# Column sums of the norms closer behind their products, six FFN tiles ahead of the second norm, and the right factors in the order of need

## The chip, the cores and the metric

One Trainium2 chip, one core of it. The metric is the device time of one execution in microseconds (us), the median of several runs. TensorE (PE) multiplies and writes into banks of PSUM; VectorE (DVE), ScalarE (ACT) and GpSimd (POOL) work on tiles of 128 partitions in SBUF; SyncE (SP) issues the DMAs.

## The reference

Two layers of a decoder trunk for 1024 tokens of width 1024, all in float32:

```python
for l in range(DEPTH):
    u = rmsnorm(h, attn_norm[l])
    rq, rk, rv, rg, dq, dk, dv = split(u @ w_in[l])
    ret = silu(rg) * rmsnorm(retention_chunkwise(rq, rk, rv), ret_norm[l])
    dif = rmsnorm(diff_attention(dq, dk, dv, lam), diff_norm[l]) * (1.0 - lam_init)
    h = h + concatenate([ret, dif]) @ w_out[l]
    u = rmsnorm(h, ffn_norm[l])
    h = h + (silu(u @ w_gate[l]) * (u @ w_up[l])) @ w_down[l]
return rmsnorm(h, final_norm)
```

`rmsnorm` divides each token by the root of the mean of its squares over the 1024 channels and multiplies by a gain. The hidden width of the FFN is 2816, 22 tiles of 128.

## The kernel before

The kernel keeps h transposed, eight tiles `a` of 128 channels by 1024 tokens, and works on two halves of 512 tokens. A product in float32 is three matmuls: each factor is split in a high part (a cast by ACT) and a low part (source minus high part, by DVE or POOL): high × high, high × low, low × high. `weight`, `wsplit` (L220, L221) do it for weights, `part` (L235, L236) for the right factors.

**Gate and up** use a form with seven products in place of eight (Strassen and Winograd). For each of the 22 tiles of the hidden width, products q0 to q6 of 12 matmuls (128 x 512) run through `gate_up`: q0 (x) and q1 (y) need the first half's norm alone, q2 to q6 the right factors `b[2]` to `b[6]`, which are sums and differences of both halves' norms: t12 and t22 (the second half's norms), b11 and b21 (at first the first half's, in `keep`). `TAGS7` names the pool of tiles for each factor. Products q2, q4 and q6 go on in the bank of x, q3 and q5 in one named z. y lies in a bank "t"; the add `first` (L956) empties it, into tile `kb` or `acc`; ACT copies x (L951), and z between q3 and q5 (L951 too). The weights of the seven products come from `factors`: two raw tiles, four sums on DVE (L903 to L908, in `sums` and `last`), and seven splits.

Since the second half's norm comes late, `feed_forward` runs q0 and q1 of the first `NPRE` tiles ahead: 10 products for which PE needs no second norm. A `Line` holds the products, and `line.later(n, f)` puts an instruction of another engine behind the start of product n. So each engine has a fixed order, that in which the program issues; DVE, ACT and POOL work through their rows one by one.

**The norms** are generators that are woven into the row of matmuls: `yield n` lets n units of matmuls pass (in steps of three) before the norm's next part. `squares` has ACT square the eight tiles (L406) as the products before it update h, and DVE (two of the seven: POOL) add them into one tile `acc` (L414). `rsqrt_rows` then sums over the channels on PE (L378, matmuls with ones), works out the reciprocal root (L383 to L390), and PE transposes it back (L394), `gap` units later. `seven_first` does the first half for the FFN, `seven_second` the second, with the steps of the factors b[2] to b[6] put behind ten products in a fixed order; `norm_half` is the norm ahead of a layer's projection, and `final` the last one.

The last adds to h ahead of a norm are those of the projection (L863, h plus a bank), one for each group of products.

Of the kernel before, what the change touches and what calls it, by code (L numbers as in the profile page):

```python
# [23 lines left out]
HT = T // NH  # L24
# [3 lines left out]
NPRE = 5  # L28
# [3 lines left out]
TAGS7 = ["u", "u", "ka", "v", "sp", "u", "u"]  # L32
# [69 lines left out]
def shape_tables():  # L102
# [10 lines left out]
    kd = np.repeat(np.exp((P - 1 - c)[:, None] * lg[None, :]), 64, axis=1)  # L113
# [31 lines left out]
class Trunk:  # L145
# [29 lines left out]
    def consts(self):  # L175
# [5 lines left out]
        self.tabs = self.const("c_tabs", [P, 1026])  # L181
# [235 lines left out]
    def norm_half(self, h, hf, gcol, us, pool=True, lag=14, first=False, keep=False):  # L417
        nc = self.nc
        sl = slice(hf * HT, hf * HT + HT)
        parts = self.squares(h, sl, 0, pool, first)  # L420
        yield lag
        y = yield from self.rsqrt_rows(parts, D)
        hi = self.t("u", 4, [P, KT, HT], R32)
        lo = self.t("u", 4, [P, KT, HT], R32)
        for k in range(KT):
# [4 lines left out]
            eng = nc.gpsimd if k in ((1, 4) if keep else (1, 3, 5, 7)) else nc.vector  # L430
# [18 lines left out]
    def seven_second(self, h, gcol, b, keep, line):  # L449
# [12 lines left out]
        t2 = []  # L462
# [311 lines left out]
    def ret_scores(self, x, n):  # L774
# [17 lines left out]
        if n < 7:  # L792
# [3 lines left out]
            nc.vector.tensor_tensor(out=kd, in0=tps[:, 0:256], in1=self.tabs[:, 768:1024], op=ALU.mult)  # L796
# [16 lines left out]
    def retention(self, l, x, mix):  # L813
# [3 lines left out]
        st = self.t("acc", 1, [P, 512])  # L817
# [5 lines left out]
        for n in range(8):  # L823
# [13 lines left out]
            if n < 7:  # L837
# [4 lines left out]
                for p in range(2):  # L842
                    for j in range(2):
# [3 lines left out]
                        nc.vector.scalar_tensor_tensor(out=sv, in0=sv, scalar=self.tabs[r, 1024 + p:1025 + p], in1=kv,  # L847
# [39 lines left out]
    def factors(self, line, at, pos, early=0, tags=("wr", "wr"), mixed=False):  # L887
# [44 lines left out]
    def gate_up(self, line, at, b, pre, st, room, done, early=0):  # L932
# [4 lines left out]
        self.factors(line, at, {j: n0 + i for i, j in enumerate([range(7), range(2), range(2, 7)][pre])}, early)  # L937
# [321 lines left out]
```

## Time and profile before

| | us |
|---|---|
| median of 3 runs | 2338.24 |
| lowest, highest | 2337.26, 2345.36 |
| profiled execution | 2341.53 |
| its span | 2339.8 |
| PE busy | 2274.7 |
| DVE busy | 1390.7 |
| ACT busy | 1011.3 |
| POOL busy | 850.9 |

The profile shows one execution; its times count from the span's start. PE's matmuls overlap at their ends, so a matmul listed with 0.39 us starts 0.23 us after the one before. In the timeline, "[idle before <-releaser]" is the time in which the engine stood still ahead of an instruction, and what ended it. The granted clock is 1.00 for the full 2.4 GHz and 0.50 for 1.2 GHz. The FFN of layer 0 begins near 507 us, the boundary of the layers lies near 1180 us, and layer 1's FFN begins near 1661 us.

### The profile page before, as it was taken

What the parts mean: (1) busy time and instruction counts of PE and PEld (TensorE: products, weight loads), DVE (VectorE), ACT (ScalarE), POOL (GpSimd) and SP (SyncE); (2) the same over time, 40 slices, a digit from 0 to 9 for tenths busy, and PEclk for the clock granted to TensorE, in tenths of its full rate; (3) what the DMA queues carried; (4) which work ended last, traced back from release to release, by engine and by line L of the source; (5) the groups of instructions that cost most, each with busy time, mean ns of one, the idle gap of its engine ahead of it and who ended that gap; (6) DMA issues with size and microseconds to landing.
All of it is one profiled execution on the core that took longest, in us unless ns stands there. A gap on an engine that the chain in (4) does not pass through costs nothing. (4 is left out here: it accounts for less than half of the span.)

```text
span 2339.8 us, 30724 instructions
## 1 busy us (share of the span) xinstructions
PE 2274.7 (97%) x11328; PEld 1906.9 (82%) x11328; DVE 1390.7 (59%) x2512; ACT 1011.3 (43%) x1905; POOL 850.9 (36%) x672
## 2 busy tenths in 40 slices
PE   7999999997999999999999999999889999999998
PEld 5888898876888888888888888988768888888887
DVE  7777603968543433896557774058874444449855
ACT  5666623434333333543246665244443333345332
POOL 4111212144545455335231112212544545544351
PEclk8999999999999999999999999999999999999999
DMA  4312121101332322753232122111123232345522
GB/s 159 81 46 64 46 91 45 55 28 56 125 126 77 126 86 92 242 164 115 73 90 55 49 70 81 56 36 54 46 94 128 77 126 77 104 145 184 185 63 73
DMA packets 73926, 215.66 MB, mean 92 GB/s; under 512 B 7984, under 2 KB 10032, under 8 KB 73776
## 3 DMA queue, kind: packets, MB, share of 16 engines
q1 hardware_dynamic: 73776, 213.70, 28.5%
q8 instruction: 89, 1.46, 0.3%
q14 instruction: 61, 0.50, 0.1%
HBM read 161.24 MB, written 44.04 MB: 88 GB/s over the span
## 5 line engine op out<-in xcount | busy, mean ns | idle before, releaser
L221 POOL TENSOR_TENSOR w<-wr,w 128x512 fp32r<-128x512 f32 x302 | 430.3, 1437 | 497.9 <-ACT w L220 466.3
L261 POOL TENSOR_TENSOR w<-wr,w 128x512 fp32r<-128x512 f32 x140 | 186.6, 1339 | 576.4 <-ACT w L260 547.5
L268 PE MATMUL ps_mm<-u,w 128*128 128x512 f32 (+1 forms) x735 | 296.6, 404 | 0.0
L270 PE MATMUL ps_mm<-u,w 128*128 128x512 f32 (+1 forms) x735 | 288.0, 392 | 0.0
L269 PE MATMUL ps_mm<-u,w 128*128 128x512 f32 (+1 forms) x735 | 287.8, 392 | 0.0
L220 ACT CAST w<-wr 128x512 fp32r<-128x512 f32 x320 | 193.2, 619 | 154.3 <-DVE wr L905 74.7
L244 PE MATMUL ps_mm<-u,w 128*128 128x512 f32 x448 | 175.6, 392 | 5.6 <-DVE t L963 5.6
L246 PE MATMUL ps_mm<-u,w 128*128 128x512 f32 x448 | 174.8, 390 | 0.0
L245 PE MATMUL ps_mm<-u,w 128*128 128x512 f32 x448 | 174.8, 390 | 0.0
L270 PEld LDWEIGHTS ps_mm<-u,w 128*128 128x128 f32 x735 | 138.4, 188 | 30.4
L951 ACT COPY t<-ps_mm 128x512 f32<-128x512 f32 x80 | 47.0, 588 | 258.6 <-PE ps_mm L246 258.6
L268 PEld LDWEIGHTS ps_mm<-u,w 128*128 128x128 f32 x735 | 138.8, 189 | 24.1
L269 PEld LDWEIGHTS ps_mm<-u,w 128*128 128x128 f32 x735 | 138.8, 189 | 23.3
L260 ACT CAST w<-wr 128x512 fp32r<-128x512 f32 x140 | 86.0, 619 | 128.8 <-PE ps_t L269 38.5
L305 PE MATMUL ps_mm<-w,u 128*128 128x256 f32 x448 | 127.1, 284 | 1.0 <-DVE u L431 1.0
L303 PE MATMUL ps_mm<-w,u 128*128 128x256 f32 x448 | 127.9, 285 | 0.0
L304 PE MATMUL ps_mm<-w,u 128*128 128x256 f32 x448 | 126.8, 283 | 0.0
L863 DVE TENSOR_TENSOR a<-a,ps_mm 128x512 f32<-128x512 f32 (+1 forms) x148 | 98.7, 667 | 45.7 <-PE ps_mm L270 27.5
L577 DVE CUSTOM_DVE_ANT_0 sp<-ps_s,wr 128x512 f32<-128x512 f32 (+2 forms) x192 | 103.2, 551 | 34.3 <-PE ps_s L575 33.1
L581 ACT ACTIVATE sp<-sp,m 128x256 f32<-128x256 f32 (+7 forms) x128 | 99.2, 775 | 53.4 <-DVE m L580 52.9
L244 PE MATMUL ps_t<-u,w 128*128 128x512 f32 x256 | 104.2, 407 | 18.5 <-DVE kb L956 18.5
L903 DVE TENSOR_TENSOR t<-wr,wr 128x512 f32<-128x512 f32 x48 | 35.4, 737 | 123.0 <-DMA wr<-wts 123.0
(364 smaller groups left out, 5959.8 us busy)
## 6 DMA issues: line engine op xcount, KB each, us to landing
wr<-wts SPq DMA_DIRECT2D x192, 512.0 KB, 3.7
mx<-s_fast SPq DMA_DIRECT2D x56, 512.0 KB, 5.2
s_fast<-mx SPq DMA_DIRECT2D x48, 512.0 KB, 4.3
kb<-ka SPq DMA_DIRECT2D x64, 128.0 KB, 2.3
s_rest<-mx SPq DMA_DIRECT2D x12, 512.0 KB, 2.9
kb<-wts SPq DMA_DIRECT2D x12, 512.0 KB, 5.4
mx<-s_rest SPq DMA_DIRECT2D x12, 512.0 KB, 3.3
a<-xT SPq DMA_DIRECT2D x16, 256.0 KB, 5.4
```

The source lines that it names most:

```text
L220: nc.scalar.copy(h, src)
L221: (eng or nc.gpsimd).tensor_tensor(out=o, in0=src, in1=h.bitcast(F32), op=ALU.subtract)
L244: mm(ps, lhsT=wh[:, c], rhs=bh, start=first and i == 0, stop=False, skip_group_check=True)
L245: mm(ps, lhsT=wh[:, c], rhs=bl, start=False, stop=False, skip_group_check=True)
L246: mm(ps, lhsT=wl[:, c], rhs=bh, start=False, stop=i == 3, skip_group_check=True)
L261: nc.gpsimd.tensor_tensor(out=o, in0=raw[:, cols], in1=h.bitcast(F32), op=ALU.subtract)
L268: mm(out, lhsT=lh, rhs=rh, start=first, stop=False)
L269: mm(out, lhsT=lh, rhs=rl, start=False, stop=False)
L270: mm(out, lhsT=ll, rhs=rh, start=False, stop=last)
L303: mm(o, lhsT=uh, rhs=wh, start=k == 0, stop=False)
L304: mm(o, lhsT=uh, rhs=wl, start=False, stop=False)
L305: mm(o, lhsT=ul, rhs=wh, start=False, stop=k == KT - 1)
```

## The change

- In the FFN's norms the column sums come 12 matmuls behind the products (11 units in steps of three) where they were 33 and 18, and the transposes 9 behind them where they were 15 and 9; in the norm at the layers' boundary it is 12 and 9 where it was 15 and 15.
- POOL adds no squares; DVE adds all. `acc` has two buffers. In `norm_half` behind the first, all low parts are DVE's.
- `NPRE` is 6. x of the sixth tile lies in a bank "s"; y of the last two tiles have a bank each that is taken once ("t" and "s", `hold`), and the z of the first six tiles share the one named "s".
- `seven_second` issues its steps by the need of the products, three and then four behind each product; the low parts of t22 are DVE's.
- The raw tiles of the first full tile of weights and their sums come at the start of the FFN, and the low parts of seven named products' weights are DVE's (`own`).
- The decay table of the retention's keys is read with a broadcast (4 columns in place of 256).

```diff
-NPRE = 5
+NPRE = 6
...
-TAGS7 = ["u", "u", "ka", "v", "sp", "u", "u"]
+TAGS7 = ["u", "u", "ka", "v", "u", "u", "sp"]
...
-            s = (tmp() if k else self.t("acc", 1, [P, 512]))[:, :n]
+            s = (tmp() if k else self.t("acc", 2, [P, 512]))[:, :n]
...
-                    eng = nc.gpsimd if pool and k in (2, 4) else nc.vector
-                    eng.tensor_tensor(out=acc, in0=acc, in1=s, op=ALU.add)
+                    nc.vector.tensor_tensor(out=acc, in0=acc, in1=s, op=ALU.add)
...
+        parts = self.squares(h, sl, 0, True, first)
         yield lag
-        y = yield from self.rsqrt_rows(parts, D)
+        y = yield from self.rsqrt_rows(parts, D, gap=gap)
...
-            eng = nc.gpsimd if k in ((1, 4) if keep else (1, 3, 5, 7)) else nc.vector
+            eng = nc.gpsimd if keep and k in (1, 4) else nc.vector
...
-        parts = self.squares(h, slice(0, HT), 0, True)
-        yield 32
-        y = yield from self.rsqrt_rows(parts, D)
+        parts = self.squares(h, slice(0, HT), 0)
+        yield 11
+        y = yield from self.rsqrt_rows(parts, D, gap=9)
...
-        parts = self.squares(h, sl, 0, True)
-        yield 16
+        parts = self.squares(h, sl, 0)
+        yield 11
...
-        b += [self.views(tag) for tag in TAGS7[2:4]]
...
+        b += [self.views(TAGS7[2]), self.views(TAGS7[3]), None, self.views(TAGS7[5]), None]
+        two = [self.big("sp") for _ in range(2)]
+        t2 = [two[i // 2][:, c[i % 2]] for i in range(4)]
...
+        def sub(out, x, z, q=None, i=0):
+            v(out=out, in0=x, in1=z, op=ALU.subtract)
+            if q is not None:
+                nc.scalar.copy(b[q][i][0], out)
...
-            b22 = self.views(TAGS7[5])
-            for i in range(4):
-                norm(t22[i], 4 + i)
-                self.part(t22[i], b22[i], nc.gpsimd)
-            yield
...
-                low(t2[i], b[2][i])
-                nc.scalar.copy(b[3][i][0], b11[i])
-            yield
-            for i in range(4):
-                low(b11[i], b[3][i])
-            yield
-            for i in range(4):
-                v(out=b21[i], in0=b21[i], in1=t2[i], op=ALU.subtract)
-            yield
-            b.append(self.views(TAGS7[4]))
-            for i in range(4):
-                v(out=b11[i], in0=t22[i], in1=t12[i], op=ALU.subtract)
-                nc.scalar.copy(b[4][i][0], b11[i])
...
-        go = steps()
-        for q in range(10):
-            line.later(line.n + q, lambda: next(go))
+        r = range(4)
+        ops = [lambda i=i: norm(t12[i], i) for i in r]
+        ops += [lambda i=i: norm(t22[i], 4 + i) for i in r]
+        for i in r:
+            ops.append(lambda i=i: sub(b11[i], t12[i], b11[i]))
+            ops.append(lambda i=i: sub(t2[i], t22[i], b11[i], 2, i))
+        ops += [lambda i=i: low(t2[i], b[2][i]) for i in r]
+        ops += [lambda i=i: self.part(b11[i], b[3][i], nc.vector) for i in r]
...
+        ops += [lambda i=i: sub(b11[i], t22[i], t12[i]) for i in r]
+        ops += [lambda i=i: self.part(t22[i], b[5][i], nc.vector) for i in r]
+        ops.append(lambda: room(4))
+        ops += [lambda i=i: self.part(b11[i], b[4][i], nc.vector) for i in r]
+        ops += [lambda i=i: sub(b21[i], b21[i], t2[i]) for i in r]
+        ops.append(lambda: room(6))
+        ops += [lambda i=i: self.part(b21[i], b[6][i], nc.vector) for i in r]
+        for i, op in enumerate(ops):
+            line.later(line.n + (i // 3 if i < 21 else 7 + (i - 21) // 4), op)
...
-            line.w[n] = self.wsplit(src, self.nc.vector if mixed and n % 3 == 0 else None)
+            line.w[n] = self.wsplit(src, self.nc.vector if n in own else None)
...
-            put(pos[2] - 4 - early, load, 0)
-            put(pos[2] - 3 - early, load, 1)
-            put(pos[2] - 1 - early, sums)
-            put(pos[2] - 1 - early, last)
+            n = pos[2] - LEAD
+            n0, n1, n2 = early or (n - 4, n - 3, n - 1)
+            line.later(n0, lambda: load(0))
+            line.later(n1, lambda: load(1))
+            line.later(n2, sums)
+            line.later(n2, last)
...
-                    st[name] = self.bank(tag)
+                    st[name] = st.pop("bank_" + name, self.bank)(tag)
...
-        tiles = {}
+        tiles, held = {}, {}
+
+        def hold(tag):
+            if tag not in held:
+                held[tag] = self.bank(tag)
+            return held[tag]
...
-            st[t]["tag"] = ["mm", "mm", "mm", "o", "t"][t]
+            st[t]["tag"] = ["mm", "mm", "mm", "o", "t", "s"][t]
             self.gate_up(line, at + 2 * t, b, 1, st[t],
-                         lambda t=t: g[t] if t < 4 else self.t("acc", 1, [P, 512]), None)
+                         lambda t=t: g[t] if t < 4 else self.t("acc", 2, [P, 512]), None, own=range(4, 2 * NPRE, 2))
+            if t > 3:
+                st[t]["bank_y"] = lambda tag, t=t: hold("ts"[t % 2])
+            st[t]["bank_z"] = hold
...
+            kw = {"early": (-1, -1, 0), "tags": ("sp", "sp"), "own": range(2 * NPRE, 2 * NPRE + 5, 2)} if t == 0 else {}
+            self.gate_up(line, at + 2 * t, b, 2 if t < NPRE else 0, st[t], room, done(t), **kw)
...
-        norm0 = self.norm_half(h, 0, 0, us, False, keep=True)
-        norm1 = self.norm_half(h, 1, 0, us, False, 8, True)
+        norm0 = self.norm_half(h, 0, 0, us, keep=True, gap=14)
+        norm1 = self.norm_half(h, 1, 0, us, 8, 14, True)
```

PE, ahead of the FFN of layer 0: L378 are the column sums of the first half, ps_mm the groups of the projection that end with an add to h. Before:

```order
2449 L268 MATMUL ps_mm_865_4776<-u_682_3876,w_829_4581 128x512
2450 L269 MATMUL ps_mm_865_4776<-u_683_3877,w_829_4581 128x512
2451 L270 MATMUL ps_mm_865_4776<-u_682_3876,w_830_4582 128x512
2452 L378 MATMUL ps_s_867_4787<-c_ones_74,acc_855_4725 128x1 x4
2453 L268 MATMUL ps_mm_865_4776<-u_682_3876,w_829_4581 128x512
2454 L269 MATMUL ps_mm_865_4776<-u_683_3877,w_829_4581 128x512
2455 L270 MATMUL ps_mm_865_4776<-u_682_3876,w_830_4582 128x512
2456 L268 MATMUL ps_mm_869_4803<-u_682_3876,w_831_4585 128x512
```

and now:

```order
2428 L268 MATMUL ps_mm_863_4748<-u_682_3876,w_824_4571 128x512
2429 L269 MATMUL ps_mm_863_4748<-u_683_3877,w_824_4571 128x512
2430 L270 MATMUL ps_mm_863_4748<-u_682_3876,w_825_4572 128x512
2431 L378 MATMUL ps_s_865_4762<-c_ones_74,acc_855_4725 128x1 x4
2432 L268 MATMUL ps_mm_867_4775<-u_682_3876,w_826_4575 128x512
2433 L269 MATMUL ps_mm_867_4775<-u_683_3877,w_826_4575 128x512
2434 L270 MATMUL ps_mm_867_4775<-u_682_3876,w_827_4576 128x512
2435 L268 MATMUL ps_mm_867_4775<-u_682_3876,w_826_4575 128x512
```

The sums stood 33 matmuls behind the last group of their half (its end is row 2418 of before), now 12; that is 21 places.

DVE, in the FFN of layer 0: L956 of before and L940 of now is the same add, which empties the bank of y (kb_876 is the place of tiles 2 and 3, acc that of tile 4). L469 of before is the low part of a factor, L496 and L500 differences; now L469 are differences, L474 and L236 low parts of factors and L221 those of weights. Before:

```order
771 L956 TENSOR_TENSOR kb_876_4907<-ps_t_935_5111,t2_934_5109 128x512
772 L469 TENSOR_TENSOR ka_914_5021<-sp_932_5101,ka_912_5019 128x512 x2
773 L469 TENSOR_TENSOR ka_915_5022<-sp_933_5102,ka_913_5020 128x512 x2
774 L469 TENSOR_TENSOR v_918_5025<-mx_841_4607,v_916_5023 128x512 x2
775 L469 TENSOR_TENSOR v_919_5026<-mx_842_4608,v_917_5024 128x512 x2
776 L956 TENSOR_TENSOR kb_876_4907<-ps_t_942_5162,t2_941_5160 128x512
777 L496 TENSOR_TENSOR mx_843_4609<-mx_843_4609,sp_932_5101 128x512 x2
778 L496 TENSOR_TENSOR mx_844_4610<-mx_844_4610,sp_933_5102 128x512 x2
779 L500 TENSOR_TENSOR mx_841_4607<-u_911_5018 128x512 x2
780 L500 TENSOR_TENSOR mx_842_4608<-u_911_5018 128x512 x2
781 L956 TENSOR_TENSOR acc_958_5240<-ps_t_951_5211,t2_950_5209 128x512
```

and now:

```order
781 L940 TENSOR_TENSOR kb_876_4907<-ps_t_936_5105,t2_935_5103 128x512
782 L221 TENSOR_TENSOR w_941_5141<-wr_934_5096,w_940_5140 128x512
783 L469 TENSOR_TENSOR sp_920_5022<-u_909_5011,mx_842_4608 128x512
784 L474 TENSOR_TENSOR ka_912_5014<-sp_919_5021,ka_910_5012 128x512 x2
785 L474 TENSOR_TENSOR ka_913_5015<-sp_920_5022,ka_911_5013 128x512 x2
786 L236 TENSOR_TENSOR v_916_5018<-mx_841_4607,v_914_5016 128x512
787 L940 TENSOR_TENSOR kb_876_4907<-ps_t_943_5150,t2_942_5148 128x512
788 L221 TENSOR_TENSOR w_948_5186<-sp_888_4930,w_947_5185 128x512
789 L236 TENSOR_TENSOR v_916_5018<-mx_841_4607,v_914_5016 128x512
790 L236 TENSOR_TENSOR v_917_5019<-mx_842_4608,v_915_5017 128x512 x2
791 L469 TENSOR_TENSOR mx_841_4607<-u_909_5011 128x512 x2
792 L469 TENSOR_TENSOR mx_842_4608<-u_909_5011 128x512 x2
```

Between the adds of y of tiles 2 and 3 stood eight low parts; now there are one low part of a weight, one difference, four low parts of ka and one of v.

ACT, a little later: L951 of before and L935 of now copy x (ps_mm) and z (ps_s) of the first full tile. L507 of before and L235 of now are casts of factors, L220 of weights. Before:

```order
477 L507 CAST u_962_5263<-mx_843_4609 128x512 x2
478 L507 CAST u_962_5263<-mx_844_4610 128x512 x2
479 L951 COPY t2_963_5272<-ps_mm_896_4953 128x512
480 L336 ACT_TABLE_LOAD
481 L336 ACTIVATE kb_875_4906<-kb_875_4906 128x512
482 L220 CAST w_965_5288<-wr_945_5179 128x512
483 L951 COPY t2_967_5296<-ps_s_964_5275 128x512
```

and now:

```order
482 L935 COPY t2_968_5304<-ps_mm_898_4957 128x512
483 L336 ACT_TABLE_LOAD
484 L336 ACTIVATE kb_875_4906<-kb_875_4906 128x512
485 L220 CAST w_969_5319<-wr_953_5215 128x512
486 L235 CAST sp_971_5323<-mx_843_4609 128x512 x2
487 L235 CAST sp_972_5324<-mx_844_4610 128x512
488 L935 COPY t2_975_5333<-ps_s_961_5252 128x512
```

The copy of z stands behind the first three casts of the seventh factor now (sp_971 and sp_972); before, behind those of the sixth.

## Rows read from the trace of the kernel before

**Rows 1.** The page, busy us (share of the span) and instructions of an engine.
```profile
PE 2274.7 (97%) x11328; PEld 1906.9 (82%) x11328; DVE 1390.7 (59%) x2512; ACT 1011.3 (43%) x1905; POOL 850.9 (36%) x672
```

**Rows 2.** Waits of PE: engine line waited for: us, times, longest.
```profile
PE ps_t L244 <- DVE kb L956: 18.5, 4, 5.1
PE ps_s L378 <- DVE acc L414: 12.1, 6, 3.5
PE ps_mm L244 <- DVE t L963: 5.6, 2, 2.8
```

**Rows 3.** Windows by stage: stretch, length, busy (instructions) PE PEld DVE ACT POOL, clock, DMA.
```profile
511.00:569.50 58.50, 44.30 (x166) 34.82 (x164) 51.98 (x63) 27.05 (x49) 31.58 (x20) 0.85 0.16 47
1665.00:1724.00 59.00, 44.28 (x172) 34.43 (x171) 54.84 (x65) 27.05 (x49) 31.63 (x20) 0.88 0.18 50
569.50:700.00 130.50, 130.25 (x571) 107.28 (x572) 60.13 (x84) 45.89 (x82) 62.99 (x46) 1.00 0.35 121
```

**Rows 4.** Windows behind five waits of PE, same columns.
```profile
514.00:520.50 6.50, 6.50 (x22) 5.52 (x23) 1.35 (x5) 1.59 (x5) 4.66 (x4) 0.50 0.18 42
541.20:544.50 3.30, 3.30 (x10) 2.56 (x9) 3.30 (x5) 3.30 (x7) 1.92 (x2) 0.50 0.07 27
548.00:554.70 6.70, 4.45 (x11) 3.48 (x12) 6.70 (x10) 1.47 (x3) 1.04 (x1) 0.50 0.27 78
569.60:576.00 6.40, 6.25 (x27) 5.18 (x28) 3.73 (x7) 1.59 (x3) 1.30 (x1) 1.00 0.42 145
1179.50:1186.00 6.50, 5.45 (x17) 4.71 (x18) 1.56 (x5) 0.41 (x2) 3.72 (x4) 0.50 0.72 245
```

**Rows 5.** PE's instructions: start, us, line, tiles, count, [idle before, releaser].
```profile
491.92 0.95 PE L378 MATMUL ps_s<-c_ones,acc 128*128 128x1 f32 x8
511.46 0.39 PE L246 MATMUL ps_t<-u,w 128*128 128x512 f32 x1
513.93 1.41 PE L378 MATMUL ps_s<-c_ones,acc 128*128 128x1 f32 x6 [2.08 <-DVE acc L414]
540.52 0.50 PE L244 MATMUL ps_t<-u,w 128*128 128x512 f32 x1 [4.14 <-DVE kb L956]
550.25 0.79 PE L244 MATMUL ps_t<-u,w 128*128 128x512 f32 x1 [5.12 <-DVE kb L956]
569.75 0.50 PE L244 MATMUL ps_mm<-u,w 128*128 128x512 f32 x1 [2.80 <-DVE t L963]
1180.55 1.84 PE L378 MATMUL ps_s<-c_ones,acc 128*128 128x1 f32 x8 [3.48 <-DVE acc L414]
```

**Rows 6.** DVE's instructions, same columns.
```profile
486.07 0.69 DVE L414 TENSOR_TENSOR acc<-acc,t 128x512 f32<-128x512 f32 x1 [0.75 <-ACT t L406]
511.25 0.67 DVE L863 TENSOR_TENSOR a<-a,ps_mm 128x512 f32<-128x512 f32 x1
516.87 0.16 DVE L390 SCALAR_TENSOR_TENSOR ny<-nx,ny 128x4 f32<-128x4 f32 x1
520.70 2.72 DVE L465 SCALAR_TENSOR_TENSOR u<-a,c_gains,ps_s 128x512 f32<-128x512 f32 x4 [1.44 <-PE ps_s L394]
543.89 5.70 DVE L469 TENSOR_TENSOR v<-mx,v 128x512 fp32r<-128x512 f32 x4
550.12 2.48 DVE L496 TENSOR_TENSOR mx<-mx,sp 128x512 f32<-128x512 f32 x4
569.02 0.68 DVE L963 TENSOR_TENSOR t<-ps_mm,t 128x512 f32<-128x512 f32 x1
1174.04 3.47 DVE L414 TENSOR_TENSOR acc<-acc,t 128x512 f32<-128x512 f32 x2 [0.88 <-POOL acc L414]
```

**Rows 7.** POOL's low parts, one alone and the first of three beside DVE.
```profile
487.88 1.29 POOL L221 TENSOR_TENSOR w<-wr,w 128x512 fp32r<-128x512 f32 x1 [7.74 <-ACT w L220]
544.20 1.51 POOL L221 TENSOR_TENSOR w<-wr,w 128x512 fp32r<-128x512 f32 x1 [1.38 <-ACT w L220]
```

**Rows 8.** ACT's copy out of the bank of z.
```profile
561.17 0.58 ACT L951 COPY t<-ps_s 128x512 f32<-128x512 f32 x1
```

More of the change, by code (lines that the diff above doesn't have):

```diff
@@ L396, in rsqrt_rows, with squares @@
         return out[:, :cols]
-    def squares(self, h, sl, alone, pool, first=False):
+    def squares(self, h, sl, alone, kb=False, first=False):
         nc = self.nc
-        tmp = (lambda: self.big("kb")[:, 0:512]) if first else self.tmp
+        tmp = (lambda: self.big("kb")[:, 0:512]) if kb else self.tmp
         n = sl.stop - sl.start
@@ L412, in squares, with norm_half @@
                 else:
-                    eng = nc.gpsimd if pool and k in (2, 4) else nc.vector
-                    eng.tensor_tensor(out=acc, in0=acc, in1=s, op=ALU.add)
+                    nc.vector.tensor_tensor(out=acc, in0=acc, in1=s, op=ALU.add)
         return parts
-    def norm_half(self, h, hf, gcol, us, pool=True, lag=14, first=False, keep=False):
+    def norm_half(self, h, hf, gcol, us, lag=11, gap=9, first=False, keep=False):
         nc = self.nc
         sl = slice(hf * HT, hf * HT + HT)
-        parts = self.squares(h, sl, 0, pool, first)
+        parts = self.squares(h, sl, 0, True, first)
         yield lag
-        y = yield from self.rsqrt_rows(parts, D)
+        y = yield from self.rsqrt_rows(parts, D, gap=gap)
         hi = self.t("u", 4, [P, KT, HT], R32)
@@ L795, in ret_scores @@
                 nc.tensor.transpose(out=tps[:, P * p:P * p + P], in_=rk[p][:, cs], identity=self.ident)
-            nc.vector.tensor_tensor(out=kd, in0=tps[:, 0:256], in1=self.tabs[:, 768:1024], op=ALU.mult)
+            heads = lambda t: t.rearrange("p (h c) -> p h c", h=4)
+            nc.vector.tensor_tensor(out=heads(kd), in0=heads(tps[:, 0:256]),
+                                    in1=heads(self.tabs[:, 768:772]).broadcast_to([P, 4, 64]), op=ALU.mult)
         return sd, kd
@@ L816, in retention @@
         mm = nc.tensor.matmul
-        st = self.t("acc", 1, [P, 512])
+        st = self.t("acc", 2, [P, 512])
         nc.gpsimd.memset(st, 0.0)
@@ L846, in retention @@
                         sv = state[p][r, P * j:P * j + P]
-                        nc.vector.scalar_tensor_tensor(out=sv, in0=sv, scalar=self.tabs[r, 1024 + p:1025 + p], in1=kv,
+                        nc.vector.scalar_tensor_tensor(out=sv, in0=sv, scalar=self.tabs[r, 772 + p:773 + p], in1=kv,
                                                        op0=ALU.mult, op1=ALU.add)
@@ L885, in out_diff, with factors @@
                     yield from self.down_group(h, w, f, hf, 4, rhs, "mm")
-    def factors(self, line, at, pos, early=0, tags=("wr", "wr"), mixed=False):
+    def factors(self, line, at, pos, early=None, tags=("wr", "wr"), own=()):
         v = self.nc.vector.tensor_tensor
@@ L930, in factors, with gate_up @@
             put(pos[6], split, pos[6], 1, 1)
-    def gate_up(self, line, at, b, pre, st, room, done, early=0):
+    def gate_up(self, line, at, b, pre, st, room, done, **kw):
         nc = self.nc
@@ L936, in gate_up @@
         n0 = len(line.products)
-        self.factors(line, at, {j: n0 + i for i, j in enumerate([range(7), range(2), range(2, 7)][pre])}, early)
+        self.factors(line, at, {j: n0 + i for i, j in enumerate([range(7), range(2), range(2, 7)][pre])}, **kw)
         def go(name, tag, q):
@@ L1075, in down_fast @@
         for e in range(2):
-            self.factors(line, at + 2 * e, {j: n0 + 2 * j + e for j in range(7)}, 0,
-                         [RAWS[(m + e) % 5], RAWS[(m + 2 + e) % 5]], True)
+            self.factors(line, at + 2 * e, {j: n0 + 2 * j + e for j in range(7)}, None,
+                         [RAWS[(m + e) % 5], RAWS[(m + 2 + e) % 5]],
+                         [n for n in range(n0, n0 + 14) if n % 3 == 0])
         def go(st, name, tag, q, n):
@@ L1170, in final @@
         sl = slice(c0, c0 + n)
-        parts = self.squares(h, sl, alone, True)
+        parts = self.squares(h, sl, alone)
         yield 14
```

31 lines of the change are left out of this document (4 added, 27 removed).

## The prediction

> **What bounds the kernel now.** I read the busy table first: PE works 97% of a span of 2339.8 us [rows 1], so a gain can only come from the places where PE stands still or runs slowly. The list of PE's waits shows them: adds of squares that column sums wait for (L378), adds that empty the banks of y (L956), and one add of the first full tile (L963) [rows 2]. Then the windows by stage. In the middle of the FFN, 571 matmuls take 130.5 us, a pace of 0.2285 us, 2.74 us for a product of 12 [rows 3]. The first 58.5 us of layer 0's FFN hold 166 matmuls, 12 of them column sums and transposes of about 1.5 us together: 154 × 0.2285 + 1.5 = 36.7 us of work, so 21.8 us are lost; layer 1's 59 us hold 172, 38.1 us of work, and lose 20.9 us [rows 3]. PE's single instructions and the granted clock say how. Four waits of 2.08, 4.14, 5.12 and 2.80 us make 14.1 us [rows 5], and after three of them the clock is granted at 0.50, the 1.2 GHz level, for 6.50, 3.30 and 4.45 us of busy time, half of which is lost: 7.1 us [rows 4]. Together 21.2 us, which agrees. At the boundary of the layers a wait of 3.48 us [rows 2] and half of 5.45 us at 0.50 [rows 4] make 6.2 us.
>
> So the change touches 21.8 + 20.9 + 6.2 = 48.9 us, and a little at the end. All of these waits end with a DVE instruction. DVE is busy for 51.98 of the 58.5 us [rows 3]; what orders its queue decides.
>
> **Column sums 11 units behind the products.** For the first half of layer 0 the sum moves 21 matmuls forward (33 to 12): 491.92 − 21 × 0.2285 = 487.12 [rows 5]. Its last add of squares ends at 486.07 + 0.69 = 486.76 [rows 6], so it need not wait. The transposes behind it come 4.8 + 1.4 = 6.2 us earlier (9 matmuls behind the sum, not 15), and with them the 16 norm instructions of that half. They stood among the last adds of the projection: the one at 511.25 [rows 6] came 3.7 us after its group on PE, which ended 18 matmuls before the sum's place at 511.69 (last matmul 511.46 + 0.23 [rows 5]), at 507.6. Freed, it ends at 508.4, and with the 0.75 us to the next add of squares and that add's 0.69 us [rows 6] the sum of the second half is ready at 509.8. Its place moves 6 matmuls to 510.3. That would be no wait, but the two squares that POOL added now stand on DVE too (1.4 us). I take 0.8 us, with bounds of 0 and the present 2.08.
>
> **Steps by need, on a fuller DVE.** From 520.70 to 569.02 DVE now does 52 instructions in 48.3 us, 0.93 us each. Without company one costs 0.68 us (2.72/4, read from a bank) or 0.62 us (2.48/4, SBUF alone) [rows 6]. The rest is POOL: four subtractions that took 5.70 us stood beside three low parts on POOL [rows 6, 7], (5.70 − 2.48)/3 = 1.07 us each. The new queue, from the first low part behind the norm to the last low part of the seventh factor, has 65: 44 steps (four more, since POOL gives up the parts of t22), 7 low parts of weights that were POOL's, 8 sums of weights and 6 adds of y. It starts about 2.2 us behind the sum's place, at 512.5 (now the sum starts at 513.93 and the last row of the statistics ends at 517.03, 3.1 us, half of them at half clock [rows 5, 6]). POOL has about 7 low parts left in that time.
>
> Who waits, with the products of this FFN counted from 0, of which 0 lies ahead of the sum, and with PE's places counted from 510.3 (product n starts at 510.3 + (n − 1) × 2.74 + 1.55, the sum and the transposes):
> - Product 9, y of tile 4, takes the bank that the add of y of tile 3 empties. That add is the 33rd instruction: 512.5 + 8 × 0.68 + 25 × 0.62 + 3 × 1.07 = 536.7, against a place at 533.8: 2.9 us. Now products 8 and 9 wait 4.14 and 5.12 us [rows 5].
> - Product 13, the first z, takes the bank of y of tile 5, whose add is the 52nd: 512.5 + 5.4 + 44 × 0.62 + 6 × 1.07 = 551.6, against 544.7.
> - Product 15 needs the first z copied out by ACT, which in ACT's queue stands behind casts that wait for the last subtractions, DVE's 61st: 512.5 + 5.4 + 53 × 0.62 + 7 × 1.07 = 558.3, and 1.2 us for cast and copy (the copy is 0.58 [rows 8]): 559.5, against 550.2.
>
> Each takes in the one before, so the sum is 559.5 − 550.2 = 9.3 us, with 0.8 for the column sum. What half clock comes before product 15 hides in its wait; behind it I add 2.0 us, the mean of what followed the five waits here (3.25, 1.65, 2.2, 0 and 2.7 us of loss [rows 4]). That makes 12.1 us against 21.8 and 20.9: gains of 9.7 and 8.8 us.
>
> By bounds: without any company the 61st ends at 550.8, which leaves product 15 a loss of 1.8, with the column sum 2.6 and with half clock up to 5; at today's 0.93 us each it ends at 569.2, a loss of 20.2 + 2.8 = 23.0 us.
>
> On POOL's price the Trainium skill ("SBUF — State Buffer", section "SBUF: two separate sides") says that the port pair that DVE and GpSimd share is locked for a whole instruction and the other blocks. By that rule a POOL low part would cost DVE its full 1.29 us alone [rows 7], not the 1.07 us above: 1.5 us more per layer, 3 us in all. The rows bear out the direction and not the full size.
>
> **Boundary, ends, the rest.** At the boundary two adds of squares took 3.47 us from 1174.04 on, behind an add on POOL [rows 6]. On DVE alone at 0.69 each they would end at 1175.4 with the same start, and the last add of the projection, 0.67 behind them, and the last add of squares (0.75 + 0.69 later) at 1177.5; without the 0.88 us of idle time for POOL, at 1176.6. The sum's place is 1180.55 − 3.48 − 3 × 0.2285 = 1176.4 [rows 5]. That leaves 0.2 to 1.1 us of waiting; I take 0.8, and 0.5 for a clock that may fall: 1.3 against 6.2, a gain of 4.9. At the program's end two POOL adds leave the chain of the squares: 0.5 us, between 0 and 1.3 (a POOL instruction alone is 1.29 [rows 7]); at its start POOL added no squares, and I count nothing. The decay table read with a broadcast keeps its one DVE instruction, and attention's other waits stay; I cost them at nothing, between −1 and +1 us. One bank for z in six tiles gives a copy or add one or two products' time (2.74 or 5.5 us) for 0.58 to 0.68 us of work [rows 6, 8]: nothing, unless DVE is late.
>
> **The sum.** 9.7 + 8.8 + 4.9 + 0.5 = 23.9 us. The profiled execution took 2341.5 us (span 2339.8), 3.3 above the median of 2338.2: 2341.5 − 23.9 = 2317.6 for a profiled run, and 2338.2 − 23.9 = 2314 as median.
>
> **Rivals.**
> A. DVE runs nearly undisturbed, and the clock does not fall: losses of about 5 per FFN, −16.8 − 15.9 − 5.4 = −38, so 2300. For it: a 2.80 us wait at 569.75 was followed by full clock [rows 4, 5]. Against: three others of like length were not.
> B. The shortening of the queue is eaten: DVE stays at 0.93 us an instruction, because adds wait in turn for PE's products and lows for ACT's casts. 23.0 per FFN loses 3.3 us, and the boundary and the end gain 5.4: 2336, no change. At 0.85 us it is 18.2 per FFN: 2326. For it: 13 more instructions. Against: POOL's share of the contention falls by more than half.
> C. DVE becomes the bound, on the slower side. While three POOL instructions ran, an instruction took 1.43 us [rows 6]. If moved casts and lows wait for one another in DVE's strict row so that its mean is 1.05 us, the 61st ends at 576.6 and FFN loses 27.6 + 2.8 = 30.4 us: 8.6 + 9.5 − 5.4 = +13, so 2351. It decides from 0.95 us on (24.3 us lost per FFN, 2.5 + 3.4 more, which eat the 5.4). Against: all the pairs with POOL would have to stay.
> D. The early sums of the norm wait for their adds, as 3.48 us does now, since they stand closer behind the products: all six at 2 us and half clock after each lose about 2 us more than forecast at four places, +8: 2322.
>
> On the clock: of the four waits in layer 0's first window, the one of 2.80 us was followed by full clock and the three others by 0.50 [rows 4, 5]. The Trainium skill ("TensorE: Matmul & The Clock Gate", section "HAM oscillation — how this bites in real kernels") describes this as a cost that is paid anew at each idle gap long enough to cool the engine. By that rule all three new waits would be followed by half clock; what follows products 9 and 13 vanishes in the next wait, and behind product 15 it would be 2.7 us, 0.7 us a layer more than above.
>
> **How the numbers follow.** Forecast 0.55; A 0.17; B 0.14 (half of it at 2326 and half at 2336); C 0.05; D 0.09. Leaving out the upper part of B, C and the fast tail of A gives 2300 to 2328. What a measurement can tell here is about 0.5%, 11.7 us: faster means below 2326.5. The forecast, A, D and a little of B lie there: 0.85; same 0.10, the rest of B and of D; slower 0.05, C.
>
> **What would show it right or wrong.** Right: the waits on L956's successor shrink to one of about 3 us per layer, with one on the z bank and one on ACT's copy behind it; the column sums wait under 1 us at four places; the first FFN window has about 12 us less than full pace, not 21.8; DVE's 65 instructions take about 48 us. Wrong: a mean DVE instruction over 0.85 us there, a new wait on the bank of z in each tile, or half clock for over 6 us behind the last wait.

## The result and the profile after

The changed kernel takes 2317.4 us (median of 4 runs, 2316.4 to 2319.02) against 2339.34 us of the kernel before (median of 4): ratio 0.9903, 95% interval 0.9883 to 0.9923, 22 us or 0.9% less. Forecast were 2314 and a gain of 24. The total came out near, but by terms that missed in both directions.

The page, and the waits of PE that answer to [rows 2] (engine, line waited for: us in total, times, longest):

```profile
PE 2265.0 (98%) x11328; PEld 1900.0 (82%) x11328; DVE 1389.3 (60%) x2564; ACT 1010.4 (44%) x1905; POOL 781.0 (34%) x620
```
```profile
PE ps_s L378 <- DVE acc L413: 8.2, 4, 4.1
PE ps_t L244 <- ACT t L935: 5.7, 2, 2.8
...
PE ps_s L244 <- DVE acc L940: 3.4, 2, 2.5
PE ps_s L244 <- ACT t L935: 3.4, 2, 1.7
...
PE ps_mm L244 <- DVE t L947: 1.1, 2, 0.6
```

The 18.5 us on the adds that empty y's banks, L956 of before, are gone; 5.7 + 3.4 + 3.4 + 1.1 us stand in the same stretch. The line of the column sums, 12.1 us before, still has 8.2: 4.06 at the boundary, the rest at the program's start and end. PE's and ACT's single instructions in layer 0's FFN, at the boundary, and products 9 and 13 of layer 1 (1677.84 and 1691.48), against [rows 5]:

```profile
509.51 1.02 PE L378 MATMUL ps_s<-c_ones,acc 128*128 128x1 f32 x8
...
535.78 0.47 PE L244 MATMUL ps_t<-u,w 128*128 128x512 f32 x1 [2.84 <-ACT t L935]
...
549.41 0.47 PE L244 MATMUL ps_s<-v,w 128*128 128x512 f32 x1 [0.89 <-DVE acc L940]
...
556.82 0.50 PE L244 MATMUL ps_s<-u,w 128*128 128x512 f32 x1 [1.70 <-ACT t L935]
...
560.40 0.50 PE L244 MATMUL ps_mm<-sp,w 128*128 128x512 f32 x1 [0.56 <-DVE t L947]
...
1166.06 1.20 PE L378 MATMUL ps_s<-c_ones,acc 128*128 128x1 f32 x5 [4.06 <-DVE acc L413]
...
1677.84 0.47 PE L244 MATMUL ps_t<-u,w 128*128 128x512 f32 x1 [2.85 <-ACT t L935]
...
1691.48 0.47 PE L244 MATMUL ps_s<-v,w 128*128 128x512 f32 x1 [2.52 <-DVE acc L940]
...
556.19 0.58 ACT L935 COPY t<-ps_s 128x512 f32<-128x512 f32 x1
```

The column sum at 509.51 waits for nothing now. Products 9, 13, 15 and 16 of layer 0 wait 2.84, 0.89, 1.70 and 0.56 us. At the boundary the sum waits 4.06 us, more than the 3.48 of before. DVE's row in the same FFN, from the first low part behind the norm to the add behind the last low part, against [rows 6]:

```profile
511.63 0.17 DVE L390 SCALAR_TENSOR_TENSOR ny<-nx,ny 128x4 f32<-128x4 f32 x1
511.75 0.69 DVE L221 TENSOR_TENSOR w<-wr,w 128x512 fp32r<-128x512 f32 x1
...
534.95 0.68 DVE L940 TENSOR_TENSOR kb<-ps_t,t 128x512 f32<-128x512 f32 x1
...
548.59 0.68 DVE L940 TENSOR_TENSOR acc<-ps_s,t 128x512 f32<-128x512 f32 x1
...
552.64 3.59 DVE L469 TENSOR_TENSOR mx<-mx,sp 128x512 f32<-128x512 f32 x4
556.15 3.59 DVE L236 TENSOR_TENSOR sp<-mx,sp 128x512 fp32r<-128x512 f32 x4
559.66 0.68 DVE L947 TENSOR_TENSOR t<-ps_mm,t 128x512 f32<-128x512 f32 x1
```

The row of 65 instructions runs from 511.75 to 559.66: 47.9 us, 0.74 us each. Before, 52 took 48.3 us.

To see where the time went, take the distance from each matmul to the next, less the usual (median) distance behind a matmul of that line and shape, and add up what exceeds 0.15 us (time lost by PE, us):

| | start | FFN 0 | boundary | FFN 1 | end | all |
|---|---|---|---|---|---|---|
| before | 13.5 | 21.0 | 5.6 | 20.8 | 2.9 | 83.6 |
| after | 10.0 | 8.3 | 6.0 | 8.5 | 3.9 | 56.4 |

The losses shrink by 27.2 us and the span by 25.2 (2339.8 to 2314.6); the difference was not traced. The two FFNs give 25.0 of it, the start 3.5; the boundary and the end give nothing and take 1.4.

### The profile page after: what moved, and what is told of

Same layout as the page of the kernel before. It is cut to its first block, busy times and chain, and to the rows that moved or that the text cites. A ratio compares the mean times of both kernels' runs of the same rounds, so it can differ in the third digit from the quotient of the medians.

```text
span 2314.6 us, 30688 instructions
## 1 busy us (share of the span) xinstructions
PE 2265.0 (98%) x11328; PEld 1900.0 (82%) x11328; DVE 1389.3 (60%) x2564; ACT 1010.4 (44%) x1905; POOL 781.0 (34%) x620
## 4 chain that ended last, share of the span: by engine, by line
PE 82%; DVE 12%; ACT 3%; issue 2%; DMA 1%; POOL 0%; SPq 0%; DVEq 0%; ACTq 0%; POOLq 0%
PE ps_mm L244 8%; PE ps_mm L246 8%; PE ps_mm L245 8%; PE ps_mm L268 7%; PE ps_mm L269 7%; PE ps_mm L270 7%; PE ps_s L244 5%; PE ps_s L246 5%; PE ps_s L245 5%; PE ps_mm L305 2%; PE ps_mm L303 2%; PE ps_mm L304 2%; PE ps_t L246 2%; PE ps_t L245 2%; PE ps_t L244 2%
## 5 line engine op out<-in xcount | busy, mean ns | idle before, releaser
L221 POOL TENSOR_TENSOR w<-wr,w 128x512 fp32r<-128x512 f32 x286 | 401.9, 1417 | 532.1 <-ACT w L220 492.1
L261 POOL TENSOR_TENSOR w<-wr,w 128x512 fp32r<-128x512 f32 x140 | 184.7, 1326 | 576.9 <-ACT w L260 550.5
L220 ACT CAST w<-wr 128x512 fp32r<-128x512 f32 x312 | 188.1, 619 | 134.5 <-DVE wr L887 72.0
L245 PE MATMUL ps_mm<-u,w 128*128 128x512 f32 x432 | 168.3, 390 | 0.0
L246 PE MATMUL ps_mm<-u,w 128*128 128x512 f32 x432 | 168.2, 389 | 0.0
L244 PE MATMUL ps_mm<-u,w 128*128 128x512 f32 x432 | 168.2, 389 | 0.0
L935 ACT COPY t<-ps_mm 128x512 f32<-128x512 f32 x76 | 44.6, 587 | 254.0 <-PE ps_mm L246 254.0
L260 ACT CAST w<-wr 128x512 fp32r<-128x512 f32 x140 | 85.9, 619 | 133.9 <-PE ps_mm L269 42.8
L244 PE MATMUL ps_s<-u,w 128*128 128x512 f32 x264 | 102.9, 390 | 3.4 <-ACT t L935 3.4
```

Source lines behind the costliest of these rows:

```text
L220: nc.scalar.copy(h, src)
L221: (eng or nc.gpsimd).tensor_tensor(out=o, in0=src, in1=h.bitcast(F32), op=ALU.subtract)
L244: mm(ps, lhsT=wh[:, c], rhs=bh, start=first and i == 0, stop=False, skip_group_check=True)
L245: mm(ps, lhsT=wh[:, c], rhs=bl, start=False, stop=False, skip_group_check=True)
L246: mm(ps, lhsT=wl[:, c], rhs=bh, start=False, stop=i == 3, skip_group_check=True)
L261: nc.gpsimd.tensor_tensor(out=o, in0=raw[:, cols], in1=h.bitcast(F32), op=ALU.subtract)
```

## The experiments

Each was timed in three rounds beside the kernel before; the medians and these losses of PE (as in the table above) came out. The runs were made in three sets; the kernel before took 2340.3, 2339.8 and 2339.9 us beside them and 2339.3 beside the changed kernel, so the sets are compared as they stand, to about 1 us:

| run | us | FFN 0 | boundary | FFN 1 | end |
|---|---|---|---|---|---|
| own_pool | 2322.95 | 11.9 | 6.1 | 10.7 | 3.9 |
| own_all | 2324.94 | 10.9 | 6.2 | 11.7 | 3.9 |
| lows_pool | 2315.72 | 8.5 | 5.8 | 9.1 | 3.9 |
| bw_dve | 2314.16 | 9.1 | 1.7 | 8.4 | 3.9 |
| before_places | 2341.04 | 20.6 | 5.6 | 20.5 | 2.9 |
| before_sq_only | 2339.82 | 21.6 | 4.8 | 20.9 | 2.8 |
| before_sq | 2330.49 | 17.8 | 5.8 | 17.6 | 2.9 |
| old_places | 2324.48 | 12.7 | 6.1 | 12.6 | 3.9 |
| old_steps | 2324.40 | 12.7 | 5.8 | 12.0 | 4.1 |
| npre5 | 2334.03 | 16.8 | 6.0 | 15.3 | 4.0 |
| best1 | 2312.26 | 8.4 | 1.7 | 9.1 | 2.9 |
| best3 | 2316.11 | 9.9 | 1.7 | 10.5 | 2.9 |

**What the low parts cost on which engine: own_pool, own_all.**

```diff
-  own=range(4, 2 * NPRE, 2)           "own": range(2 * NPRE, 2 * NPRE + 5, 2)
+  (own_pool) none of them on DVE
+  (own_all)  own=range(3, 2 * NPRE)   "own": range(2 * NPRE, 2 * NPRE + 5)
```

> The changed kernel with the low parts of the weights of seven products at the FFN's start back on POOL, all else as changed. Theory 1 (the FFN's start is bound by DVE's row, in which a low part on DVE costs 0.62 us and one on POOL costs DVE about 1.1 us by contention): the row loses 7 x 0.62 = 4.3 us and gains 7 x 1.1 = 7.7, so product 16 starts 3.4 us later in each layer: +7 us, 2324. Rival (DVE's number of instructions counts, POOL's work is free): 4.3 us less in each layer, 2309.

> The changed kernel with the low parts of all weights of products 3 to 16 on DVE, none on POOL in the stretch of the FFN's start. Theory 1: about 7 low parts leave POOL, 7 x (1.1 - 0.62) = 3.4 us less in DVE's row per layer: 2311. Rival (number of DVE's instructions): 7 x 0.62 = 4.3 us more per layer: 2326.

own_pool lost 5.5 us to the changed kernel, as theory 1 has it (+7) and against the rival (−8). own_all lost 7.5 us: theory 1 expected a gain, and the rival's number, 2326, is the nearer one. Two things in its DVE row speak against counting a price of 1.1 us for each POOL instruction. A low part of a weight now stands among the adds of squares ahead of the second half's sum (first line). And in a strict row a low part waits for ACT's cast, and the row with it (the other two); the row of layer 0 takes 49.0 us in place of 47.9.

```profile
501.80 1.77 DVE L221 TENSOR_TENSOR w<-wr,w 128x512 fp32r<-128x512 f32 x1
...
530.14 0.69 DVE L221 TENSOR_TENSOR w<-wr,w 128x512 fp32r<-128x512 f32 x1 [1.69 <-ACT w L220]
...
536.36 0.69 DVE L221 TENSOR_TENSOR w<-wr,w 128x512 fp32r<-128x512 f32 x1 [0.49 <-ACT w L220]
```

In layer 0 the loss is the sum's: it costs 1.7 us (0.3 in the changed kernel) and 1.5 us of half clock behind it; the whole FFN loses 2.6 us more (10.9 for 8.3). So seven low parts on DVE are better than none of them (by 5.5 us) and better than all (by 7.5); own_all doesn't tell the price of a low part behind the sum.

**The boundary: lows_pool, bw_dve.**

```diff
 (lows_pool)
-  eng = nc.gpsimd if keep and k in (1, 4) else nc.vector
+  eng = nc.gpsimd if k in ((1, 4) if keep else (1, 3, 5, 7)) else nc.vector
 (bw_dve) in first_weights, the weights of the next layer's projection
-  self.weight()
+  self.weight(eng=self.nc.vector)
```

> The changed kernel with four of the eight low parts of the norm ahead of a layer's projection back on POOL (the squares stay on DVE). At the layers' boundary the column sum waits 4.06 us in the changed kernel. Theory 2 (it waits because DVE's row there is full, and POOL's contention is what fills it): 4 low parts less on DVE (-2.5 us), 4 more on POOL (+4.4 us): the wait grows to about 6 us, +2 to +3 us, 2319.5. Rival (the low parts moved to DVE are what kept the wait): 2.5 us less of it and less half clock, wait about 1.5 us, 2313.

> The changed kernel with the low parts of the next layer's first weights, which POOL makes at the boundary beside DVE's adds and norms, on DVE; DVE's row takes most of them behind the last add of squares. Theory 2: the adds lose the contention of 6 low parts and the wait of the column sum (4.06 us) falls under 1 us, with the half clock behind it: -4 to -6 us, 2312, unless the weights come too late for the projection (then a wait on them of up to 2 us). Rival (the sum waits since it stands too close behind the products): no change of the wait.

lows_pool changed next to nothing there (5.8 us lost for 6.0): both expectations missed, a low part costs the adds about as much on the one engine as on the other. bw_dve hit at the boundary: with POOL's low parts of the weights gone the sum does not wait, and 1.7 us are left, a wait on the weights. That wait moved the sum back, but does not decide: without the 1.7 us the sum's place would be 1163.0 (1164.72 less 1.7, an estimate), and its last add ends at 1162.88. The 4.3 us saved there are within the 4 to 6 expected; the medians differ by 3.2. The adds in the changed kernel (first fence), with POOL beside them, and the same adds and the new wait in bw_dve:

```profile
1155.55 3.09 DVE L430 TENSOR_TENSOR u<-t,u 128x512 fp32r<-128x512 f32 x2 [0.59 <-ACT u L428]
1158.56 1.77 DVE L413 TENSOR_TENSOR acc<-acc,kb 128x512 f32<-128x512 f32 x1
...
1165.23 0.68 DVE L413 TENSOR_TENSOR acc<-acc,kb 128x512 f32<-128x512 f32 x1
...
1156.63 1.45 POOL L261 TENSOR_TENSOR w<-wr,w 128x512 fp32r<-128x512 f32 x1 [0.26 <-ACT w L260]
1158.05 1.73 POOL L261 TENSOR_TENSOR mx<-wr,mx 128x512 fp32r<-128x512 f32 x1
```
```profile
1155.46 1.29 DVE L430 TENSOR_TENSOR u<-t,u 128x512 fp32r<-128x512 f32 x2
1156.67 0.68 DVE L413 TENSOR_TENSOR acc<-acc,kb 128x512 f32<-128x512 f32 x1
...
1162.19 0.69 DVE L413 TENSOR_TENSOR acc<-acc,kb 128x512 f32<-128x512 f32 x1
...
1162.33 0.50 PE L270 MATMUL ps_mm<-u,w 128*128 128x512 f32 x1 [1.51 <-DVE w L261]
...
1164.72 0.95 PE L378 MATMUL ps_s<-c_ones,acc 128*128 128x1 f32 x8
```

Two low parts took 3.09 us beside POOL and 1.29 without; an add of squares 1.77 and 0.68.

**The parts of the FFN's gain, alone and taken back.**

```diff
 (before_places) the kernel before, with
-  yield 32 ... rsqrt_rows(parts, D)          yield 16
+  yield 11 ... rsqrt_rows(parts, D, gap=9)   yield 11
 (before_sq_only) the kernel before, with
-  eng = nc.gpsimd if pool and k in (2, 4) else nc.vector
+  eng = nc.vector
 (before_sq) both
 (old_places) the changed kernel, with yield 32 and 16, lag and gap 14
 (old_steps) the changed kernel, with the steps of seven_second and TAGS7 of before, "early": (2, 3, 5)
 (npre5) the changed kernel, with NPRE = 5, no held banks, steps at line.n + i // 4, "early": (0, 1, 3)
```

> The kernel before with only the FFN's column sums and transposes at their new places (12 matmuls behind the products, transposes 9 behind them), all else as before. Theory 1 (DVE's row sets when PE goes on, so an earlier start of the row is a gain as a whole): the waits on the sum (2.1 to 2.3 us) and the half clock behind it go, 4.4 and 4.1 us, and the row starts about 1.4 to 3 us earlier against PE's products: -6 to -7 us per layer, 2326. Rival (the places save the sum's wait alone, the row's order decides the rest): -8 us in all, 2332.

> The kernel before with all adds of squares on DVE and the sums at their old places. Theory 3: the sum is ready about 2 to 3 us earlier, so most of its wait of 2.1 us and the half clock go: -3 us per layer, 2333. Rival (the norm instructions of the first half, late at the old places, keep the sum late whoever adds): 2339.

> The kernel before with the FFN's column sums at their new places (as in the run before_places, which gained nothing) and all adds of squares on DVE (none on POOL, everywhere). Theory 3 (the adds of squares form one chain, and its two visits to POOL, not the sum's place, made the sum wait: in before_places it still waited 2.47 us): the wait and the half clock behind it go, and DVE's row starts about 5 us earlier than before: -5 us per layer, 2329. Rival (places and squares do nothing without the sixth tile): 2339.

Alone, neither the places (1.0007, interval 0.9997 to 1.0017) nor the squares on DVE (0.9995, 0.9985 to 1.0005) gain anything; together they gain 9.4 us (0.9955, 0.9940 to 0.9970). Both expectations for before_places missed. before_sq_only came out where its rival had it (2339) and before_sq near its theory (2329). The trace of before_places shows what holds the sum: its adds go from DVE to POOL and back, and each leg costs: an add takes 1.30 and 1.61 us on POOL, 0.68 on DVE alone, and DVE's row stands still for 0.87 us behind the first.

```profile
499.67 1.30 POOL L414 TENSOR_TENSOR acc<-acc,t 128x512 f32<-128x512 f32 x1 [0.89 <-DVE acc L414]
...
501.00 1.76 DVE L414 TENSOR_TENSOR acc<-acc,t 128x512 f32<-128x512 f32 x1 [0.87 <-POOL acc L414]
...
502.90 1.61 POOL L414 TENSOR_TENSOR acc<-acc,t 128x512 f32<-128x512 f32 x1 [0.69 <-DVE acc L414]
...
512.53 1.84 PE L378 MATMUL ps_s<-c_ones,acc 128*128 128x1 f32 x8 [2.47 <-DVE acc L414]
```

The sum still waits 2.47 us, with half clock behind it. In before_sq_only it waits 0.44 us, but the norm of the first half, at its old place, fills DVE until 510.97 and the reciprocal root behind it is slow (its last three rows 0.82, 1.21 and 1.19 us beside POOL):

```profile
510.29 0.68 DVE L236 TENSOR_TENSOR u<-mx,u 128x512 fp32r<-128x512 f32 x1
...
512.43 1.21 DVE L389 TENSOR_TENSOR nx<-nx,ny 128x4 f32<-128x4 f32 x1
513.68 1.19 DVE L390 SCALAR_TENSOR_TENSOR ny<-nx,ny 128x4 f32<-128x4 f32 x1
...
515.67 0.75 DVE L465 SCALAR_TENSOR_TENSOR u<-a,c_gains,ps_s 128x512 f32<-128x512 f32 x1 [0.21 <-PE ps_s L394]
```

The first norm row of the second half in before_places, then in before_sq:

```profile
519.31 2.72 DVE L465 SCALAR_TENSOR_TENSOR u<-a,c_gains,ps_s 128x512 f32<-128x512 f32 x4 [3.68 <-PE ps_s L394]
```
```profile
514.52 2.72 DVE L465 SCALAR_TENSOR_TENSOR u<-a,c_gains,ps_s 128x512 f32<-128x512 f32 x4 [1.38 <-PE ps_s L394]
```

Counted from the first matmul of product 0, this row starts at 13.1 us in layer 0 and 12.0 in layer 1 of before, at 12.1 and 12.1 with the places alone, at 10.9 and 10.8 with the squares alone, and at 6.8 in both layers with both. So one cause stood behind the other: most of the move needs both at once. Why the 1.2 to 2.2 us that the squares alone give save no time is not shown.

> The changed kernel with all column sums and transposes of the FFN's and the boundary's norms back at their old places, all else as changed. Theory 1 (what counts is when DVE's row starts): it starts 1.4 us (6 places) to 3 us later against PE: +1.5 to +3 us per layer, 2322. Rival (the places carry the gain): the waits of before on the sum with half clock come back, +4 us or more per layer, 2327.

> The changed kernel with the factors' steps in the fixed order of before (low parts of t22 on POOL, factor pools as before, raw tiles of the first full tile a few products later), all else as changed. Theory 1 (the row's length decides, the order within it only which product waits): four instructions less on DVE (-2.5 us), four more on POOL (+3 to +4.4 us): +1 to +2 us per layer, 2320. Rival (the order by need is what saved the waits on y's banks, 9.3 us per layer): +8 to +10 us per layer, 2335.

> The changed kernel with five tiles ahead in place of six: 10 products instead of 12 before the right factors are needed, banks of y and z as before, the steps four behind each product throughout, and the raw tiles of the first full tile two products later. Theory 1: the row of DVE keeps its 48 us, PE has two products (5.5 us) less to fill them: +5.5 us per layer, +11, 2328. Rival (PE waits for the banks of y, not for the row's end): within 2 us of the changed kernel.

Taken back one by one from the changed kernel, the places cost 7.1 us, the order of the steps 7.0, and the sixth tile 16.6 (the last with a new pace of the steps and later raw tiles too, so it is not the sixth tile alone). Together that is more than the whole gain: the prices overlap.

old_places lay in the middle between its two expectations, and its trace shows neither. The FFN's sums don't wait; the transposes behind the second half's sum do, 2.54 us in layer 0 and 2.53 in layer 1. At the old places the four sums of weights (512.48 to 516.41) stand ahead of the reciprocal root in DVE's row:

```profile
515.72 0.69 DVE L890 TENSOR_TENSOR sp<-sp 128x512 f32<-128x512 f32 x1
516.33 0.15 DVE L383 TENSOR_SCALAR nx<-ps_s 128x4 f32<-128x4 f32 x1
...
517.70 0.62 PE L394 MATMUL ps_s<-c_ident,ny 128*128 128x128 f32 x4 [2.54 <-DVE ny L390]
```

For old_steps both missed, theory 1 by 4 us and the rival by 11. The waits on the adds of y are back, as the rival had it (first line below; 18.5 us in before), but the waits behind them are nearly gone. For npre5 theory 1 had the direction, but 11 us for 16.6; there too the adds of y are the wait again:

```profile
PE ps_t L244 <- DVE kb L959: 15.8, 4, 5.3
```
```profile
PE ps_t L244 <- DVE kb L940: 16.6, 4, 5.6
...
PE ps_mm L244 <- DVE t L947: 6.5, 2, 4.3
```

**A better version: best1, best3.**

```diff
 (best1) bw_dve, and in final
-  parts = self.squares(h, sl, alone)
+  parts = self.squares(h, sl, alone, pool=(2, 4))
 (best3) best1, the last steps of seven_second all behind product 13, and for the second full tile, with its first splits two and one products later
-  line.later(line.n + (i // 3 if i < 21 else 7 + (i - 21) // 4), op)
+  line.later(line.n + (i // 3 if i < 21 else min(7 + (i - 21) // 4, 12)), op)
+  if t == 1: kw = {"early": (2 * NPRE - 3, 2 * NPRE - 2, 2 * NPRE + 3), "lead": 2}
```

> The changed kernel with the low parts of the next layer's first weights on DVE (as in the run bw_dve, boundary loss 1.7 us there against 6.0) and the third and fifth square of the last norm added on POOL again. At the program's end the add of squares that waits for ACT stands ahead of the reciprocal root on DVE and costs 1.1 us in the changed kernel: that goes. bw_dve's 2314.2 less 1 us: 2313. Rival (the end's loss is not that add's): 2314.

> The run best1 with the four sums of the second full tile's weights (2.9 us on DVE) moved behind the low parts of the seventh factor, and these low parts all behind product 13 of the list. Theory 1 (PE goes on at the end of DVE's row): the row up to those low parts ends 2.9 us earlier, the waits of products 15 and 16 (1.8 and 0.7 us) go: -2.5 us per layer, 2307, unless product 17's weights come late (up to 1.5 us). Rival (these waits are ACT's, whose casts stay): 2312.

best1 is the fastest, 2312.26 us (ratio 0.9881 to before, 0.9865 to 0.9898), 5 us below the changed kernel. The two were not timed side by side and the intervals of their ratios overlap (0.9883 to 0.9898), but every run of best1 (2311.59 to 2312.97) lies below every run of the changed kernel. The end's loss is back at 2.9 us, as theory 1 had it. best3 did what was expected up to product 16 (5.6 and 5.7 us lost from product 9 on, some 3 less than in best1) and lost 4.1 and 4.6 us a few products later, where theory 1 had allowed 1.5: the raw tiles are held longer, the load of the next tile's weights is issued at 565.27 (562.33 in best1), and DVE waits 4.81 us for it.

```profile
553.18 2.49 DVE L236 TENSOR_TENSOR sp<-mx,sp 128x512 fp32r<-128x512 f32 x4
...
568.90 0.69 DVE L886 TENSOR_TENSOR t<-wr,wr 128x512 f32<-128x512 f32 x1 [4.81 <-DMA wr<-wts]
```

## Why the prediction was right, and where it was wrong

**Column sums in the FFN: right, for a reason not seen.** Forecast 0.8 us of waiting, measured none at 509.51 in layer 0 (0.3 us lost). But the prediction counted the two squares that go from POOL to DVE as 1.4 us of load against the sum. They are what frees it: before_places, with the places alone, waited 2.47 us and gained nothing.

**The DVE row: right.** 65 instructions were to take 48.3 us, from 512.5 on; they took 47.9 from 511.75 on. Product 9's wait was put at 2.9 us and is 2.84; the add it was blamed on ends at 535.63 and ACT's copy that the profile names at 535.68, so which of the two is last stays open. Product 15's chain (subtractions, casts, copy of z) is the one forecast: subtractions to 556.23, copy from 556.19 on, product at 556.82. It was put at 559.5. The subtractions ended 2.1 us earlier than counted (0.75 of it the row's start), and the copy stands behind three of the four casts, so it did not wait for the last subtraction and the 1.2 us behind that became 0.6. PE's places were right: less all losses since the sum, product 15 would have started at 549.5; put at 550.2, with a sum 0.8 us later than it came. The 9.3 us forecast for products 9 to 15, half clock in between included, were 7.3 in layer 0 (5.9 of waiting, 1.4 of half clock) and 7.5 in layer 1; product 16 adds 0.7 in each, which was not counted.

**The term that was too large: half clock behind the last wait, 2.0 us.** None came, in either layer; the other reading that the prediction gave, half clock behind the waits of products 9, 13 and 15, came for one of the six. Windows of the changed kernel behind product 9's wait in layer 0, behind product 15's, and behind product 9's in layer 1, where the wait ended at 1677.84 (columns as in [rows 3]):

```profile
536.60:540.00 3.40, 3.40 (x10) 2.67 (x9) 3.40 (x5) 2.19 (x5) 1.38 (x1) 0.52 0.21 84
556.80:566.00 9.20, 8.62 (x36) 6.79 (x37) 5.71 (x9) 3.19 (x6) 6.06 (x4) 1.00 0.27 73
1678.00:1684.00 6.00, 6.00 (x27) 4.98 (x27) 6.00 (x9) 3.30 (x7) 1.72 (x1) 1.00 0.18 70
```

The clock fell to 0.52 after 2.84 us of waiting in layer 0 and stayed at 1.00 after 2.85 us in layer 1; after 1.70 and 0.56 us it stayed too. Product 9 has this same wait in both layers of lows_pool, bw_dve, best1 and best3 as well: of the ten waits of 2.84 or 2.85 us eight were followed by the lower level. It matters little there, as the prediction had it ("hides in its wait"): in the changed kernel product 13 waits 0.89 us where the clock fell and 2.52 where it stayed, and the losses from product 9 to product 13 are 5.5 and 5.7 us (5.5 to 6.3 in the other four runs).

The loss per FFN was 8.3 and 8.5 us against 12.1 forecast. In layer 0 the column sum lost 0.3 for 0.8, products 9 to 15 7.3 for 9.3, the half clock behind them 0 for 2.0, product 16 0.7 for 0. The gain of the two FFNs was 6.5 us more than forecast; 7.4 less were lost than forecast, but this way of counting gives before 0.9 us less loss than the prediction did.

**The step that failed: the boundary.** "That leaves 0.2 to 1.1 us of waiting; I take 0.8", a gain of 4.9: measured 6.0 us lost against 5.6. It went along the last three adds alone. DVE's row there is full long before: norm, low parts, adds to h and squares stand almost without a gap from 1142 to 1165.91, beside eight low parts on POOL. bw_dve takes those away, and 4.3 us of the loss go.

**The end: wrong in sign.** A gain of 0.5 was forecast, 1.0 us was lost. The adds that POOL did ran beside the reciprocal root; on DVE one of them waits for ACT ahead of it (transposes wait 0.96 us at 2298.79). best1 puts them back, and the loss is 2.9 again.

**The start: not forecast.** It was counted at nothing and lost 3.5 us less in the profile. The start of a run varies: 9.1 to 12.4 us in ten profiles of kernels with the changed start, 10.0 to 13.8 in four with the old one. So the two traces don't show that the change does it, and no run takes the new reading of the decay table back by itself.

The sum: FFNs −25.0 for −18.5, boundary +0.4 for −4.9, end +1.0 for −0.5, start −3.5 for 0. The forecast of the total was near by luck: too little on the FFNs and too much on the boundary and the end offset each other. What was right by its mechanism is the FFN's list of waits.

**The rivals.** B and C needed a mean of 0.85 and 0.95 us on DVE; it was 0.74. A's undisturbed DVE did not come, but its full clock did, behind the last waits of layer 0 and behind every wait of layer 1. Of the sums that were moved closer only the boundary's waits as D has it, 4.06 us, and bw_dve shows that DVE's row and not the place makes it wait.

## What to carry to other kernels

A wait that ends on a full engine has the next cause right behind it: two edits that gain nothing alone gained 9.4 us together here, so try them together before dropping either. Price a move between engines on the row it joins, not by the instruction: a low part on DVE costs 0.69 us (511.75 of the changed kernel) until it waits for another engine's cast at the head of a strict row. And when a chain seems to wait on its last link, look at how long its engine has been busy without a gap before.

## What the runs showed of the hardware

Beside POOL, two SBUF-to-SBUF instructions of DVE took 3.09 us (1155.55 of the changed kernel) in place of 1.29 (bw_dve), and an instruction of four elements per partition 1.21 in place of 0.16 (512.43 in before_sq_only). Waits of PE of 2.84 or 2.85 us were followed by the clock's lower level in eight of the ten FFNs of the changed kernel, lows_pool, bw_dve, best1 and best3, and not in two. Ahead of a wait that ends on another engine the lower level cost little: with it 5.5 us were lost from product 9 to 13 in layer 0 of the changed kernel, without it 5.7 in layer 1.
